# Four more weight granules by seven products, x loaded in pairs, and the first granules laid out piece by piece, in a one-core decoder layer

## The chip, the core and the metric

The kernel runs on one core of a Trainium2 chip. Five engines run their own instruction streams and wait for each other only where a semaphore says so: PE (TensorE, matrix products into PSUM banks; its weight loads are shown as PEld), DVE (VectorE), ACT (ScalarE), POOL (GpSimd) and SP (SyncE, which issues most of the DMAs). The metric is the device time of one launch in microseconds (us); lower is better. A difference below about 0.2% (1.3 us here) can't be told from no change.

## The reference

One layer for 256 tokens of width 2048, float32 throughout. A normalised x is multiplied by one wide input matrix, whose columns are cut into q, k, v, z_a (attention, 8 heads of 128), u_b, v_b, z_b (a gated unit) and two gates:

```python
h = rms_norm(x, norm_g)
proj = h @ w_in
q, k, v, z_a, u_b, v_b, z_b, g_a, g_b = jnp.split(proj, cuts, axis=-1)
q = rms_norm(q.reshape(B, S, N_ATT_HEADS, HEAD_DIM), q_norm_g)
k = rms_norm(k.reshape(B, S, N_ATT_HEADS, HEAD_DIM), k_norm_g)
att = moba_attention(q, k, v)          # 256 tokens: causal attention in one block
y_a = (att * jax.nn.silu(z_a)) @ w_proj_a
sgu = spatial_gating(jax.nn.gelu(u_b), jax.nn.gelu(v_b), sgu_norm_g, w_s, b_s)
y_b = (sgu * jax.nn.silu(z_b)) @ w_proj_b
merged = jax.nn.sigmoid(g_a) * y_a + jax.nn.sigmoid(g_b) * y_b
return x + merged @ w_out
```

Nearly all work is in the products with w_in, w_proj_a, w_proj_b and w_out, some 120 MB of weights that are read once.

## The kernel before

**Granules.** The weights are cut into 120 granules of 128 x 2048 words (1 MB), used in a fixed order (`schedule`): eight granules each for q, k, v, za, vb, ub and zb (numbers 0 to 55), then four times eight for the gates `g` followed by four for the projections `proj`, then twice eight for `out`. In this text g62 is granule 62. A granule of one of the blocks of eight holds, for one pair `kp` of 128-row blocks of the inner dimension, a 2 x 2 grid of weight blocks of 128 x 512. It meets the 2 x 2 grid of x's blocks (two inner blocks, two halves of 128 tokens).

**Halves.** A float32 factor is used as a rounded upper half (type float32r, `wh`, made by ACT) and the rest, the lower half (`wl`, made by DVE as the factor minus its upper half, in place of the raw words). One block product is three matmuls of 128 x 512 (`three`, line 421): lower x by upper weight, upper by upper, upper by lower weight. So the lower half of the weights is first read by a granule's third matmul.

**Eight or seven products.** `direct` does a granule's eight block products: 24 matmuls. `seven` does it by Winograd's form of Strassen's scheme with seven: 21 matmuls. For that the sums of weight blocks have to be made too: DVE makes the block sums (lines 265, 267, 268), ACT their upper halves `th` (L270), and DVE the lower halves `tl` (L273), beside the lower half of the words themselves (L272, for a granule by eight L238). In the blocks of `SCRATCH` the first sum (L265) is made in memory instead: SP copies a quarter of the granule to a `ring` tensor 13 granules ahead, POOL adds another quarter by an accumulating DMA 10 granules ahead, and the quarter is then loaded from the ring. `SETS` holds, for each block, which `kp` go by seven and the order of the eight.

**Banks.** A block keeps its results in two groups of four PSUM banks, `E` (sums that only the sevens make) and `L`. When the last granule by seven is done, `early` empties E (one ACT copy, four DVE additions); when the block is done, `final` empties L (four DVE additions). The next block swaps the two groups.

**Order.** Every engine's order is written out by hand. The loop at line 804 goes over the granules; while PE is given granule i, `LEADS` tells up to which granule the halves are made (i + 2 or i + 3), four buffers hold `wh` (`WHS`), three hold the sums (`TS`, `THS`), six hold raw words (`RAWS`). All else (norms, softmax, transposes, evacuations) hangs on a granule and a place in its step: "pre" is before the halves, "mid" and "late" are inside the making of the halves, "evac" and "post" behind them (`HOOKS`, `EVAC`, and `SECOND` for the second part of a transposition). An instruction that waits holds up everything behind it on its engine.

**The beginning.** SP issues x's scales and first tile, the first granule in four pieces, and then x and granules 1 to 3 alternately (lines 292 to 306). Granules 0 to 3 lie in memory as rows of 8 KB and come in pieces (four, four, two, two) of 128 rows of 2 KB or 4 KB. `split_x` scales a pair of x's tiles and makes its halves. `load_nat` loads x once more, by rows, for the mean squares (`stats`); `forms_4`, `forms_5`, `forms` make the sums of x's blocks that the sevens need, for kp 4, kp 5, and kp 0 to 3; `halves_4` makes the halves of those of kp 4.

Of the kernel before, what the change touches and what calls it, by code (L numbers as in the profile page):

```python
# [22 lines left out]
P = 128  # L23
# [7 lines left out]
WORDS = 2048  # L31
# [12 lines left out]
SETS = {("q", 0): ((), (0, 1, 2, 3, 4, 5, 6, 7)), ("k", 0): ((0, 1, 2, 3, 4), (5, 1, 4, 3, 6, 0, 2, 7)),  # L44
# [7 lines left out]
        ("out", 0): ((0, 1, 2, 4), (3, 0, 2, 6, 1, 5, 4, 7)),  # L52
        ("out", 1): ((0, 1, 2, 3, 4), (5, 0, 1, 2, 3, 4, 6, 7))}
SCRATCH = ("za", "vb", "ub", "zb", "g", "out")
LEADS = {("q", 0): (3, 2, 2, 3, 3, 3, 3, 2), ("k", 0): (2, 3, 3, 2, 2, 2, 2, 2),
# [18 lines left out]
HOOKS = [
# [13 lines left out]
    ("za", 0, 3, "mid", "soft_exp", 0), ("v", 0, 4, "evac", "root", "k", 3), ("zb", 0, 3, "mid", "spatial"),  # L88
    ("ub", 0, 1, "evac", "squares", "vb", 0), ("q", 0, 4, "post", "forms_5"),
    ("za", 0, 5, "post", "soft_sum", 0), ("ub", 0, 3, "evac", "squares", "vb", 1),  # L90
    ("g", 0, 0, "mid", "func", "zb", AF.Silu), ("ub", 0, 5, "post", "norm", "vb", 1),
# [9 lines left out]
    ("za", 0, 3, "post", "soft_max", 1), ("vb", 0, 4, "post", "load_mix"),
    ("ub", 0, 0, "post", "turn_z", "za", "E"), ("proj", 3, 2, "mid", "halves_h", "m"),
    ("vb", 0, 2, "post", "attend", 1, "E23"), ("k", 0, 4, "late", "root", "q", 3),
    ("zb", 0, 2, "mid", "func", "ub", AF.Gelu_apprx_tanh), ("za", 0, 4, "post", "soft_sum", 1),
    ("ub", 0, 4, "evac", "root", "vb", 1), ("g", 0, 5, "post", "gate_b"), ("za", 0, 2, "post", "soft_max", 0),
    ("proj", 2, -1, "post", "func", ("g", 2), AF.Sigmoid), ("proj", 3, 0, "post", "turn_m", 2, (0, 1), "L01"),
    ("proj", 0, 1, "mid", "func", ("g", 0), AF.Sigmoid), ("k", 0, 6, "late", "norm", "q", 3),
    ("proj", 3, 2, "post", "halves_l", "m"), ("proj", 3, 2, "post", "turn_m", 1, (0, 1), "L23"),
    ("out", 0, 0, "in", "turn_m", 3, (0, 1), "E01"), ("out", 0, 2, "late", "forms_m4"),
    ("out", 0, 2, "post", "halves_m4"), ("ub", 0, 1, "mid", "func", "vb", AF.Gelu_apprx_tanh),  # L110
# [27 lines left out]
def hybrid_layer_kernel(  # L138
# [17 lines left out]
    def both(name, words, at):  # L156
# [4 lines left out]
            for i, n in ((0, 4), (1, 4), (2, 2), (3, 2))}  # L161
# [47 lines left out]
    def load_piece(i, a, b):  # L209
        nc.sync.dma_start(raw[i][:, a:b], w[i, :, a:b])  # L210
# [95 lines left out]
    load_x(12, 16)  # L306
# [439 lines left out]
    fns = dict(load_nat=load_nat, keep_vec=keep_vec, forms_4=forms_4, forms_5=forms_5, forms=forms, stats=stats,  # L746
# [33 lines left out]
    def take(i, when):  # L780
        return later.pop((i, when), [])
# [21 lines left out]
    loaded, halved = 3, 1  # L803
    for i, (kind, name, c, kp, n) in enumerate(G):
# [128 lines left out]
```

## Time and profile before

| | us |
|---|---|
| median of 3 runs | 657.42 (657.16 to 658.05) |
| the profiled execution | 657.49 |
| its span on the core | 655.8 |
| PE busy | 648.7 (99%) |
| DVE busy | 595.3 (91%) |
| ACT busy | 433.3 (66%) |
| POOL busy | 81.1 (12%) |

The span runs from the first instruction to the end of the last; the other 1.7 us of the execution lie around it. A busy share is an average over the whole span; the views by window, by wait and in order of time tell what a stage is limited by. In rows of the timeline the columns are start, duration (us), engine, line, operation, result<-operands; consecutive instructions of one engine overlap by some 0.08 us, so that the cost of one is read from start to next start.

### The profile page before, as it was taken

The page shows a single profiled execution, that of the slowest core. Times are in us where ns is not written, and L with a number is a line of the kernel's source. Part 1 is how long each engine was busy: PE and PEld are TensorE (multiplying, and loading weights), DVE is VectorE, ACT ScalarE, POOL GpSimd, SP SyncE. Part 2 cuts the span into 40 slices and gives each one's busy share as a digit, 9 for nine tenths or more (in the row PEclk, how much of TensorE's full clock was granted, in tenths as well). Part 3 has the DMA queues.
Part 4 walks back from the last instruction along what each step waited for, and adds up shares of the span by engine and source line. Part 5 has one row for each costly group of instructions (what it writes and reads, how often), then busy time and mean ns, then how long its engine had stood idle before and what let it go on. Part 6 is the DMA issues. An engine that isn't in the chain of part 4 may idle for free.

```text
span 655.8 us, 8146 instructions
## 1 busy us (share of the span) xinstructions
PE 648.7 (99%) x2968; PEld 536.6 (82%) x2968; DVE 595.3 (91%) x519; ACT 433.3 (66%) x542; POOL 81.1 (12%) x88
## 2 busy tenths in 40 slices
PE   9999999999999999999999999999999999999997
PEld 5787878888888888888888888888888888888885
DVE  4789999979978999979999998899979998999996
ACT  7869778858958678686566755564655476475660
POOL 1000522220010102300011011101101100100300
PEclk9999999999999999999999999999999999999999
DMA  8985596786685976887599679959985997986981
GB/s 298 421 351 212 194 267 228 240 259 184 207 266 156 295 227 210 256 260 283 176 292 288 210 214 320 312 196 277 310 252 193 305 296 207 271 245 223 199 285 64
DMA packets 44824, 163.14 MB, mean 249 GB/s; under 512 B 4977, under 2 KB 5617, under 8 KB 35825
## 3 DMA queue, kind: packets, MB, share of 16 engines
q1 hardware_dynamic: 35280, 145.32, 61.1%
q0 software_dynamic: 8928, 16.26, 16.3%
q10 hardware_dynamic: 576, 1.05, 0.4%
q8 instruction: 23, 0.38, 0.2%
q14 instruction: 17, 0.13, 0.1%
HBM read 157.89 MB, written 28.31 MB: 284 GB/s over the span
## 4 chain that ended last, share of the span: by engine, by line
PE 87%; DVE 6%; DMA 4%; ACT 1%; issue 1%; SPq 0%; DVEq 0%; ACTq 0%
PE acc_g L421 15%; PE y L421 13%; PE seven_g L421 10%; PE acc_out L421 9%; PE acc_vb L421 5%; PE acc_za L421 5%; PE acc_ub L421 5%; PE acc_v L421 5%; PE acc_zb L421 5%; PE seven_out L421 4%; DMA words0float<-in_w 2%; DMA cut_float<-in_w 2%; PE seven_za L421 2%; PE seven_vb L421 2%; PE seven_v L421 2%; PE seven_zb L421 2%
## 5 line engine op out<-in xcount | busy, mean ns | idle before, releaser
L222 POOL DMA_DIRECT2D ring<-in_w x48 | 40.3, 846 | 297.8 <-DMA ring<-in_w 297.6
L270 ACT CAST th<-sums0float 128x1536 fp32r<-128x1536 f32 x19 | 28.2, 1484 | 42.9 <-DVE sums0float L268 42.9
L270 ACT CAST th<-sums1float 128x1536 fp32r<-128x1536 f32 x19 | 28.2, 1484 | 38.6 <-DVE sums1float L268 37.1
L270 ACT CAST th<-sums2float 128x1536 fp32r<-128x1536 f32 x19 | 28.3, 1491 | 32.6 <-DVE sums2float L268 29.4
L421 PE MATMUL acc_g<-wh,xuh 128*128 128x512 f32 x99 | 38.6, 389 | 0.0
L421 PE MATMUL acc_g<-wh,xul 128*128 128x512 f32 x99 | 38.6, 389 | 0.0
L273 DVE TENSOR_TENSOR sums2float32r<-sums2float,th 128x1536 fp32r<-128x1536 f32 x19 | 33.3, 1752 | 2.7 <-ACT th L270 2.7
L238 DVE TENSOR_TENSOR words1float32r<-words1float,wh 128x2048 fp32r<-128x2048 f32 x13 | 29.7, 2285 | 6.3 <-ACT wh L237 6.3
L366 POOL TENSOR_TENSOR rs<-ms,mhalf 128x4 f32<-128x4 f32 x12 | 24.1, 2008 | 86.0 <-DVE ms L365 86.0
L273 DVE TENSOR_TENSOR sums1float32r<-sums1float,th 128x1536 fp32r<-128x1536 f32 x19 | 33.3, 1753 | 0.0
L273 DVE TENSOR_TENSOR sums0float32r<-sums0float,th 128x1536 fp32r<-128x1536 f32 x19 | 33.3, 1752 | 0.0
L238 DVE TENSOR_TENSOR words4float32r<-words4float,wh 128x2048 fp32r<-128x2048 f32 x13 | 29.7, 2287 | 3.7 <-ACT wh L237 3.7
L272 DVE TENSOR_TENSOR words2float32r<-words2float,wh 128x2048 fp32r<-128x2048 f32 x13 | 29.8, 2293 | 1.3
L272 DVE TENSOR_TENSOR words3float32r<-words3float,wh 128x2048 fp32r<-128x2048 f32 x11 | 25.2, 2292 | 4.7 <-ACT wh L260 3.6
L237 ACT CAST wh<-words1float 128x2048 fp32r<-128x2048 f32 x13 | 24.8, 1907 | 3.7 <-PE acc_g L421 3.7
L238 DVE TENSOR_TENSOR words5float32r<-words5float,wh 128x2048 fp32r<-128x2048 f32 x11 | 25.1, 2286 | 1.9 <-ACT wh L237 1.9
L237 ACT CAST wh<-words4float 128x2048 fp32r<-128x2048 f32 x13 | 24.9, 1917 | 1.7 <-PE y L421 1.2
L272 DVE TENSOR_TENSOR words0float32r<-words0float,wh 128x2048 fp32r<-128x2048 f32 x11 | 25.2, 2291 | 0.9
L421 PE MATMUL acc_out<-wh,ml 128*128 128x512 f32 x65 | 25.4, 391 | 0.0
L421 PE MATMUL acc_out<-wh,mh 128*128 128x512 f32 x65 | 25.3, 390 | 0.0
L421 PE MATMUL acc_q<-wh,xuh 128*128 128x512 f32 x64 | 25.1, 392 | 0.2 <-ACT wh L237 0.2
L421 PE MATMUL y<-wh,zal 128*128 128x512 f32 x64 | 25.2, 394 | 0.0
(955 smaller groups left out, 2157.0 us busy)
## 6 DMA issues: line engine op xcount, KB each, us to landing
words4float<-in_w SPq DMA_DIRECT2D x15, 1024.0 KB, 6.6
words1float<-in_w SPq DMA_DIRECT2D x14, 1024.0 KB, 7.4
words5float<-in_w SPq DMA_DIRECT2D x12, 1024.0 KB, 7.3
ring<-in_w SPq DMA_DIRECT2D x48, 256.0 KB, 7.2
ring<-in_w POOLq DMA_DIRECT2D x48, 256.0 KB, 7.4
words3float<-in_w SPq DMA_DIRECT2D x10, 1024.0 KB, 6.6
words0float<-in_w SPq DMA_DIRECT2D x9, 1024.0 KB, 6.3
words2float<-in_w SPq DMA_DIRECT2D x11, 768.0 KB, 6.4
```

Of the source, the lines that this page charges most:

```text
L222: nc.gpsimd.dma_start(pre[i], w[i, :, 2 * B:3 * B], accum_op=ALU.add)
L237: nc.scalar.copy(h, r)
L238: nc.vector.tensor_tensor(l, r, f(h), op=ALU.subtract)
L270: nc.scalar.copy(th[i], t)
L272: nc.vector.tensor_tensor(wl[i], r, f(wh[i]), op=ALU.subtract)
L273: nc.vector.tensor_tensor(tl[i], t, f(th[i]), op=ALU.subtract)
L366: nc.gpsimd.tensor_tensor(dst, ms[:, :n], mhalf[:, :n], op=ALU.pow)
L421: nc.tensor.matmul(acc, a, b, start=(start and n == 0), stop=(stop and n == 2))
```

## The change

- v, za and zb: five, five and six of eight granules go by seven products where it was four each, four more in all; the orders of kp in v, za, zb, and more slightly in k, vb, g and out, are others. The last granule of v and of za is now one by seven.
- The first loads are a list, `LOADS`: x's tiles come two pairs at a time (256 KB) at most, and granules 4 and 5 are issued ahead of x's last pair.
- Granules 0 to 3 are laid out in memory piece by piece on the host (`weight_stream`), so that each piece is one contiguous stretch; `load_piece` reads it so. The rows that arrive in SBUF are the same.
- `split_x` of the later pairs is hung on granules 0 to 3 as hooks; `load_nat` goes from behind granule 4's halves to granule 3; `forms_4` goes ahead of granule 7's halves, `forms_5` behind granule 8's.
- `LEADS`, `EVAC`, `SECOND` and the other `HOOKS` have new values: among them, the sums of v leave at the next block's first granule, and `mix`'s second part goes from "pre" to "mid".

```diff
-SETS = {... ("k", 0): ((0, 1, 2, 3, 4), (5, 1, 4, 3, 6, 0, 2, 7)),
-        ("v", 0): ((0, 1, 2, 3), (4, 5, 0, 6, 1, 2, 3, 7)), ("za", 0): ((0, 1, 2, 3), (4, 5, 0, 1, 6, 2, 3, 7)),
-        ("zb", 0): ((0, 1, 2, 3), (5, 4, 1, 0, 6, 2, 3, 7)),
-        ("g", 0): ((0, 1, 2, 3, 4), (5, 6, 3, 2, 0, 1, 4, 7)),
...
+SETS = {... ("k", 0): ((0, 1, 2, 3, 4), (5, 1, 3, 4, 6, 0, 2, 7)),
+        ("v", 0): ((0, 1, 2, 3, 4), (7, 6, 5, 4, 0, 2, 1, 3)),
+        ("za", 0): ((0, 1, 2, 3, 4), (6, 5, 3, 2, 0, 7, 4, 1)),
+        ("zb", 0): ((0, 1, 2, 3, 4, 5), (6, 1, 4, 5, 3, 2, 0, 7)),
+        ("g", 0): ((0, 1, 2, 3, 4), (5, 6, 0, 2, 4, 3, 1, 7)),
...
-         ("v", 0): (3, 2, 2, 2, 3, 3, 2, 2), ("za", 0): (2, 2, 2, 2, 2, 3, 3, 2),
-         ("zb", 0): (2, 3, 2, 2, 2, 2, 2, 2), ("g", 0): (2, 2, 3, 3, 3, 2, 2, 2),
+         ("v", 0): (2, 3, 3, 3, 3, 3, 2, 2), ("za", 0): (2, 2, 3, 3, 3, 2, 2, 2),
+         ("zb", 0): (2, 2, 2, 3, 3, 3, 2, 2), ("g", 0): (2, 2, 3, 2, 3, 2, 2, 2),
...
-        ("v", 0, "quad"): (0, "mid"),
-        ("za", 0, "early"): (1, "pre"),
+        ("v", 0, "quad"): (1, "pre"),
+        ("za", 0, "early"): (0, "pre"), ("za", 0, "quad"): (1, "pre"), ("ub", 0, "quad"): (1, "late"),
...
-SECOND = {... ("mix", 0): (1, "pre"),
+SECOND = {... ("mix", 0): (1, "mid"),
...
+    ("q", 0, 0, "pre", "split_x", 2), ("q", 0, 0, "pre", "split_x", 3),
+    ("q", 0, 1, "evac", "split_x", 5), ("q", 0, 2, "post", "split_x", 6), ("q", 0, 3, "mid", "split_x", 7),
+    ("q", 0, 1, "mid", "split_x", 4),
-    ("q", 0, 4, "post", "keep_vec"), ("q", 0, 4, "post", "forms_4"), ("q", 0, 4, "post", "forms_5"),
+    ("q", 0, 4, "pre", "keep_vec"), ("q", 0, 4, "pre", "forms_4"), ("q", 0, 5, "evac", "forms_5"),
-    ("q", 0, 4, "late", "load_nat"),
+    ("q", 0, 3, "mid", "load_nat"),
...
+LOADS = [("p", 0, 512), ("p", 512, 1024), ("x", 1, 2), ("p", 1024, 1536), ("p", 1536, 2048), ("x", 2, 4),
+         ("w", 1, 4), ("x", 4, 6), ("x", 6, 8), ("w", 2, 2), ("w", 3, 2), ("x", 8, 10), ("x", 10, 12),
+         ("x", 12, 14), ("w", 4), ("w", 5), ("x", 14, 16)]
+CUTS = {0: 4, 1: 4, 2: 2, 3: 2}
...
     def load_piece(i, a, b):
-        nc.sync.dma_start(raw[i][:, a:b], w[i, :, a:b])
+        src = w[i, :, a:b]
+        if i in CUTS:
+            n = WORDS // CUTS[i]
+            j = a // n
+            src = bass.AP(tensor=w.tensor, offset=w.offset + (i * WORDS + j * n) * P + a - j * n,
+                          ap=[[n, P], [1, b - a]])
+        nc.sync.dma_start(raw[i][:, a:b], src)
...
-    load_piece(0, 0, B)
-    load_piece(0, B, 2 * B)
-    load_x(1, 2)
-    load_piece(0, 2 * B, 3 * B)
-    load_piece(0, 3 * B, WORDS)
-    load_x(2, 4)
-    load(1, pieces=4)
-    load_x(4, 8)
-    load(2, pieces=2)
-    load_x(8, 10)
-    load(3, pieces=2)
-    load_x(10, 12)
-    load_x(12, 16)
+    for kind, *a in LOADS:
+        if kind == "x":
+            load_x(*a)
+        elif kind == "w":
+            load(*a)
+        else:
+            load_piece(0, *a)
...
-    for kp in range(1, 4):
-        split_x(kp)
-        if kp < 2:
-            split(kp, 4)
+    split_x(1)
+    split(1, 4)
...
-    loaded, halved = 3, 1
+    loaded, halved = 5, 1
...
-        if i < 4:
-            split_x(i + 4)
...
+    for i, n in CUTS.items():
+        g[i] = g[i].reshape(P, n, WORDS // n).transpose(1, 0, 2).reshape(P, WORDS)
     return np.ascontiguousarray(np.stack(g))
```

More of the change, by code (lines that the diff above doesn't have):

```diff
@@ L60 @@
+SCRATCH = ("za", "vb", "ub", "zb", "g", "out")
+LEADS = {("q", 0): (3, 2, 2, 3, 3, 3, 3, 2), ("k", 0): (2, 3, 3, 2, 3, 3, 3, 2),
[4 rows of a table added]
          ("g", 3): (2, 2, 2, 2, 2, 2, 3, 3), ("out", 0): (3, 2, 2, 3, 3, 2, 2, 2),
-         ("out", 1): (2, 2, 2, 2, 2, 2, 2, 2), ("proj", 0): (3, 2, 3, 2), ("proj", 1): (3, 2, 2, 2),
+         ("out", 1): (2, 2, 2, 2, 2, 2, 2, 3), ("proj", 0): (3, 2, 3, 3), ("proj", 1): (3, 2, 2, 2),
          ("proj", 2): (3, 3, 3, 2), ("proj", 3): (2, 3, 3, 2)}
-EVAC = {("proj", 0): (1, "late"), ("proj", 1): (1, "late"), ("proj", 2): (1, "late"), ("proj", 3): (0, "evac"),
+EVAC = {("proj", 0): (0, "evac"), ("proj", 1): (1, "late"), ("proj", 2): (0, "evac"), ("proj", 3): (0, "evac"),
@@ L64 @@
         ("g", 2, "quad"): (1, "pre"), ("zb", 0, "early"): (1, "late"), ("out", 1, "quad"): (0, "evac"),
         ("g", 3, "quad"): (0, "evac"), ("k", 0, "early"): (0, "evac"), ("vb", 0, "quad"): (0, "late"),
-        ("v", 0, "quad"): (0, "mid"), ("g", 0, "early"): (0, "late"), ("g", 1, "early"): (0, "evac"),
+        ("v", 0, "quad"): (1, "pre"), ("g", 0, "early"): (0, "late"), ("g", 1, "early"): (1, "mid"),
         ("v", 0, "early"): (0, "pre"), ("out", 1, "early"): (1, "mid"), ("out", 0, "quad"): (0, "late"),
-        ("za", 0, "early"): (1, "pre"), ("g", 3, "early"): (0, "late"), ("q", 0, "quad"): (0, "pre"),
+        ("za", 0, "early"): (0, "pre"), ("g", 3, "early"): (0, "late"), ("q", 0, "quad"): (0, "pre"),
@@ L69 @@
         ("out", 0, "early"): (1, "mid"), ("zb", 0, "quad"): (1, "pre"), ("ub", 0, "early"): (0, "evac"),
-        ("vb", 0, "early"): (0, "evac")}
-SECOND = {("turn_m", 0): (1, "late"), ("turn_m", 2): (1, "post"), ("turn_z", "za"): (1, "late"),
-          ("turn_qk", "q"): (1, "post"), ("mix", 0): (1, "pre"), ("turn_z", "zb"): (1, "post"),
+        ("vb", 0, "early"): (0, "evac"), ("za", 0, "quad"): (1, "pre"), ("ub", 0, "quad"): (1, "late"),
+        ("g", 2, "early"): (0, "late"), ("q", 0, "early"): (1, "late")}
@@ L73 @@
+SECOND = {("turn_m", 0): (1, "mid"), ("turn_m", 2): (1, "post"), ("turn_z", "za"): (1, "mid"),
+          ("turn_qk", "q"): (1, "late"), ("mix", 0): (1, "mid"), ("turn_z", "zb"): (0, "post"),
           ("turn_qk", "k"): (1, "mid"), ("turn_m", 1): (1, "pre")}
 HOOKS = [
[5 rows of a table removed]
-    ("k", 0, 1, "late", "root", "q", 1), ("proj", 0, 0, "late", "turn_z", "zb", "E23L01"),
-    ("k", 0, 1, "pre", "squares", "q", 2), ("k", 0, 3, "late", "root", "q", 2),
-    ("k", 0, 5, "late", "norm", "q", 2), ("k", 0, 3, "pre", "squares", "q", 3), ("zb", 0, 0, "post", "mix", "E"),
@@ L83 @@
-    ("proj", 3, -1, "mid", "turn_m", 0, (0, 1), "E23"), ("v", 0, 0, "mid", "squares", "k", 0),
-    ("v", 0, 1, "evac", "root", "k", 0), ("proj", 3, 0, "evac", "func", ("g", 3), AF.Sigmoid),
[3 rows of a table removed]
[L88 to L91, printed above, removed]
@@ L92 @@
-    ("ub", 0, 3, "evac", "squares", "vb", 2), ("v", 0, 3, "evac", "root", "k", 2),
-    ("ub", 0, 7, "post", "norm", "vb", 2), ("ub", 0, 4, "post", "squares", "vb", 3),
-    ("q", 0, 4, "late", "load_nat"), ("ub", 0, 7, "post", "norm", "vb", 3),
+    ("q", 0, 0, "pre", "split_x", 2), ("q", 0, 0, "pre", "split_x", 3), ("k", 0, 1, "evac", "root", "q", 2),
+    ("q", 0, 1, "evac", "split_x", 5), ("q", 0, 2, "post", "split_x", 6), ("q", 0, 3, "mid", "split_x", 7),
+    ("v", 0, 3, "late", "squares", "k", 3), ("q", 0, 4, "pre", "keep_vec"),
@@ new lines @@
+    ("ub", 0, 2, "pre", "squares", "vb", 0), ("ub", 0, 2, "evac", "squares", "vb", 1),
+    ("q", 0, 5, "post", "forms", "x", "x"), ("vb", 0, 0, "mid", "func", "za", AF.Silu),
[3 rows of a table added]
+    ("proj", 0, 0, "pre", "turn_z", "zb", "E23L01"), ("k", 0, 1, "pre", "squares", "q", 2),
+    ("v", 0, 3, "evac", "root", "k", 3), ("k", 0, 6, "post", "norm", "q", 2),
+    ("k", 0, 3, "pre", "squares", "q", 3), ("zb", 0, 0, "post", "mix", "E"),
+    ("proj", 3, -1, "mid", "turn_m", 0, (0, 1), "E23"), ("za", 0, 3, "mid", "soft_exp", 0),
@@ new lines @@
+    ("ub", 0, 4, "late", "root", "vb", 2), ("za", 0, 5, "post", "soft_sum", 0),
+    ("za", 0, 2, "late", "soft_max", 0), ("v", 0, 1, "late", "root", "k", 1),
+    ("v", 0, 3, "late", "norm", "k", 1), ("v", 0, 2, "late", "squares", "k", 2),
+    ("k", 0, 4, "evac", "root", "q", 3), ("v", 0, 5, "late", "norm", "k", 2),
+    ("v", 0, 0, "mid", "squares", "k", 0), ("q", 0, 1, "mid", "split_x", 4), ("zb", 0, 3, "late", "spatial"),
+    ("proj", 3, 0, "evac", "func", ("g", 3), AF.Sigmoid), ("ub", 0, 3, "late", "root", "vb", 0),
@@ L95 @@
+    ("g", 0, 0, "mid", "func", "zb", AF.Silu), ("ub", 0, 3, "evac", "squares", "vb", 2),
+    ("ub", 0, 6, "evac", "norm", "vb", 1), ("v", 0, 4, "late", "root", "k", 2),
+    ("ub", 0, 0, "post", "turn_z", "za", "E"), ("ub", 0, 3, "post", "squares", "vb", 3),
+    ("q", 0, 3, "mid", "load_nat"), ("q", 0, 6, "evac", "halves_h", "x"), ("ub", 0, 7, "pre", "norm", "vb", 3),
     ("v", 0, 0, "post", "turn_qk", "q", "E"), ("za", 0, 0, "post", "turn_qk", "k", "E"),
-    ("za", 0, 1, "post", "score", "E"), ("q", 0, 6, "post", "halves_l", "x"),
@@ L97 @@
-    ("ub", 0, 6, "post", "root", "vb", 3), ("ub", 0, 1, "mid", "causal_mix"),
+    ("za", 0, 1, "post", "score", "E"), ("q", 0, 6, "post", "halves_l", "x"), ("q", 0, 4, "pre", "forms_4"),
+    ("ub", 0, 5, "evac", "root", "vb", 3), ("ub", 0, 1, "pre", "causal_mix"),
     ("vb", 0, 1, "post", "attend", 0, "E01"), ("za", 0, 4, "mid", "soft_exp", 1),
-    ("ub", 0, 4, "post", "norm", "vb", 0), ("vb", 0, 0, "evac", "turn_p", 0, "E012"),
-    ("vb", 0, 0, "mid", "func", "za", AF.Silu), ("proj", 3, 1, "post", "forms", "mf", "m"),
@@ L101 @@
[L101 to L110, printed above, removed]
+    ("proj", 0, 1, "mid", "func", ("g", 0), AF.Sigmoid), ("vb", 0, 0, "late", "turn_p", 0, "E012"),
+    ("q", 0, 5, "post", "stats"), ("ub", 0, 4, "evac", "norm", "vb", 0), ("za", 0, 3, "late", "soft_max", 1),
@@ new lines @@
+    ("v", 0, 5, "late", "norm", "k", 3), ("ub", 0, 6, "evac", "norm", "vb", 2),
+    ("proj", 3, 2, "mid", "halves_h", "m"), ("vb", 0, 2, "post", "attend", 1, "E23"),
+    ("v", 0, 1, "late", "root", "k", 0), ("zb", 0, 2, "late", "func", "ub", AF.Gelu_apprx_tanh),
+    ("za", 0, 4, "post", "soft_sum", 1), ("ub", 0, 3, "evac", "root", "vb", 1),
+    ("proj", 3, 1, "post", "forms", "mf", "m"), ("q", 0, 8, "post", "halves_4"),
+    ("k", 0, 3, "evac", "norm", "q", 0), ("proj", 2, -1, "post", "func", ("g", 2), AF.Sigmoid),
@@ L111 @@
+    ("proj", 3, 0, "post", "turn_m", 2, (0, 1), "L01"), ("ub", 0, 1, "pre", "func", "vb", AF.Gelu_apprx_tanh),
+    ("k", 0, 6, "post", "norm", "q", 3), ("proj", 3, 2, "post", "halves_l", "m"),
+    ("proj", 3, 2, "post", "turn_m", 1, (0, 1), "L23"), ("out", 0, 0, "in", "turn_m", 3, (0, 1), "E01"),
+    ("out", 0, 2, "late", "forms_m4"), ("out", 0, 2, "post", "halves_m4"), ("g", 0, 5, "post", "gate_b"),
     ("vb", 0, 1, "in", "turn_p", 1, "E301"), ("proj", 1, 0, "mid", "func", ("g", 1), AF.Sigmoid),
-    ("v", 0, 5, "evac", "norm", "k", 3), ("v", 0, 1, "pre", "squares", "k", 1),
+    ("vb", 0, 3, "pre", "load_mix"), ("v", 0, 1, "pre", "squares", "k", 1), ("q", 0, 5, "evac", "forms_5"),
@@ L160, in hybrid_layer_kernel @@
     cuts = {i: [both(f"cut{i}_{j}_", WORDS // n, base + 8 * KB * i + j * 8 * KB // n) for j in range(n)]
-            for i, n in ((0, 4), (1, 4), (2, 2), (3, 2))}
+            for i, n in CUTS.items()}
     class Cut:
@@ L744, in keep_vec @@
         nc.scalar.copy(vec, vec0)
-    fns = dict(load_nat=load_nat, keep_vec=keep_vec, forms_4=forms_4, forms_5=forms_5, forms=forms, stats=stats,
+    fns = dict(split_x=split_x, load_nat=load_nat, keep_vec=keep_vec, forms_4=forms_4, forms_5=forms_5, forms=forms, stats=stats,
                halves_h=halves_h, halves_l=halves_l, halves_4=halves_4, squares=squares, root=root, norm=norm,
@@ L876, in hybrid_layer_kernel @@
             halved += 1
-            split(halved, {1: 4, 2: 2, 3: 2}.get(halved, 1), mid=lambda: run(take(i, "mid"), i), late=lambda: run(take(i, "late"), i))
+            split(halved, {2: 2, 3: 2}.get(halved, 1), mid=lambda: run(take(i, "mid"), i), late=lambda: run(take(i, "late"), i))
         run(take(i, "mid"), i)
         run(take(i, "late"), i)
-        if i < 4:
-            split_x(i + 4)
         run(take(i, "evac"), i)
```

7 lines of the change are left out of this document (3 added, 4 removed), and 23 rows, old and new, of tables (HOOKS, LEADS, SETS).

## The prediction

> **What bounds the kernel now.** I read the busy shares first, then PE's waits, then the chain of work that ended last in order of time.
>
> ```profile
> PE 648.7 (99%) x2968; PEld 536.6 (82%) x2968; DVE 595.3 (91%) x519; ACT 433.3 (66%) x542; POOL 81.1 (12%) x88
> ```
>
> PE is busy all the time by this row, but a matmul that waits half-issued is busy too, so pace has to be read from the chain:
>
> ```profile
> 15.76 13.81 DMA words0float<-in_w
> ...
> 84.50 2.72 PE seven_k L421 x12
> ...
> 93.34 5.44 PE acc_v L421 x24
> ```
>
> Up to about 30 us the end hangs on DMAs (the first row is g6's load); behind that the chain goes through ACT and DVE, which make the weights' halves, and from some 83 us on it is PE to the end. A matmul costs 2.72 / 12 = 0.227 us, so a granule by eight costs PE 24 x 0.227 = 5.44 us and one by seven 21 x 0.227 = 4.76 us. From the first matmul to v's first lie eight granules by eight (q), then five by seven and three by eight (k): 192 + 177 = 369 matmuls, 83.7 us of work.
>
> ```profile
> 5.97 0.50 PE L421 MATMUL acc_q<-wh,xuh 128*128 128x512 f32 x1 [0.17 <-ACT wh L237]
> ```
>
> PE took 93.34 - 5.97 = 87.4 us for them: 3.7 us were lost to late halves. In the window from 83 us to the end PE's waits have one row only:
>
> ```profile
> PE acc_k L421 <- DVE words2float32r L272: 0.5, 1, 0.5
> ```
>
> So from v to the end PE is the bound. That doesn't say that DVE has room. The row of the windows from 208 to 348 us, and the list of DVE's waits from 46.35 us (g9, the first granule by seven) to 348.5 us (g62, next to last of the first gate block), show how close it runs:
>
> ```profile
> 208.40:348.43 140.03, 140.03 (x644) 116.89 (x643) 132.64 (x112) 97.51 (x127) 16.74 (x18) 1.00 0.78 246
> ```
>
> ```profile
> DVE words3float32r L272 <- ACT wh L260: 3.6, 1, 3.6
> DVE v_h L476 <- ACT v_c L475: 3.0, 1, 3.0
> DVE sums2float32r L273 <- ACT th L270: 2.7, 1, 2.7
> DVE words5float32r L272 <- ACT wh L260: 2.6, 1, 2.6
> DVE words4float32r L238 <- ACT wh L237: 1.3, 1, 1.3
> DVE words5float32r L238 <- ACT wh L237: 1.0, 1, 1.0
> DVE za_h L609 <- ACT za_h L607: 0.4, 1, 0.4
> DVE zb_h L483 <- PE acc_zb L421: 0.4, 1, 0.4
> ```
>
> These are 15.0 us of idle time in 302.1. And at g62 DVE is only just in time: it ends the lower half at 346.14 + 2.29 = 348.43, and PE's third matmul reads it at 349.95:
>
> ```profile
> 46.35 0.68 DVE L265 TENSOR_TENSOR words3float<-words3float 128x512 f32<-128x512 f32 x1
> ...
> 346.14 2.29 DVE L272 TENSOR_TENSOR words2float32r<-words2float,wh 128x2048 fp32r<-128x2048 f32 x1
> ```
>
> ```profile
> 349.95 0.39 PE L421 MATMUL acc_g<-words2float32r,xuh 128*128 128x512 f32 x1
> ```
>
> The slack there is 1.52 us. The bound is thus two-fold: PE, with DVE close behind it from g9 to g62.
>
> **The four granules.** PE loses 4 x 3 = 12 matmuls, 12 x 0.227 = 2.72 us. DVE pays for it. From L265 to the next granule's L265 a granule by seven costs it 113.60 - 106.95 = 6.65 us; where the first sum comes by the ring, from L267 to L267, 326.31 - 320.38 = 5.93; one by eight, 312.59 - 310.39 = 2.20:
>
> ```profile
> 106.95 0.69 DVE L265 TENSOR_TENSOR words2float<-words2float 128x512 f32<-128x512 f32 x1
> ...
> 113.60 0.69 DVE L265 TENSOR_TENSOR words3float<-words3float 128x512 f32<-128x512 f32 x1
> ```
>
> ```profile
> 310.39 2.29 DVE L238 TENSOR_TENSOR words2float32r<-words2float,wh 128x2048 fp32r<-128x2048 f32 x1
> 312.59 2.29 DVE L238 TENSOR_TENSOR words3float32r<-words3float,wh 128x2048 fp32r<-128x2048 f32 x1
> ...
> 320.38 0.68 DVE L267 TENSOR_TENSOR sums2float<-words4float 128x512 f32<-128x512 f32 x1
> ...
> 326.31 0.69 DVE L267 TENSOR_TENSOR sums0float<-words5float 128x512 f32<-128x512 f32 x1
> ```
>
> v takes no ring: 4.45 us more. za's one and zb's two do: 3.73 each. Together 15.64 us more DVE work between g9 and g62, and 15.0 us of idle to put it in. ACT gets a `th` of 1536 words for each, at most the 1.91 us of a copy of 2048 words (row below), under 8 us in all beside 42 us of idle time in the window quoted (140.03 - 97.51). SP and POOL issue three ring copies and three adds more; the DMA share there is 0.78, and I cost them at nothing (they are issued ten and more granules ahead; at worst one load comes its own 7 us late).
>
> **The beginning of DVE's chain.** Where DVE starts on g9 decides all that follows. Now `forms_5` follows g7, and ACT's F5h holds g8's copy up behind it:
>
> ```profile
> 24.08 0.33 SPq L210 DMA_DIRECT2D words2float<-in_w  x1
> ```
>
> ```profile
> words2float<-in_w SPq DMA_DIRECT2D x1, 1024.0 KB, 10.4
> ```
>
> ```profile
> 34.88 2.29 DVE L238 TENSOR_TENSOR words1float32r<-words1float,wh 128x2048 fp32r<-128x2048 f32 x1 [0.38 <-ACT wh L237]
> ```
>
> ```profile
> 39.08 0.62 ACT L387 CAST F5h<-F 128x512 fp32r<-128x512 f32 x1 [4.12 <-DVE F L405]
> 39.60 1.91 ACT L237 CAST wh<-words2float 128x2048 fp32r<-128x2048 f32 x1
> 41.41 1.91 ACT L370 ACTIVATE xnat<-xnat 128x2048 f32<-128x2048 f32 x1
> ```
>
> After the change g8's copy needs only its load, which lands at 24.08 + 10.4 = 34.5 (the last number of the issue row), and can start when ACT is free, at 39.08 - 4.12 = 34.96; DVE, through with g7 at 37.1, then does g8 until 39.3, `forms_5` and F5h to 40.9, `forms` to 44.1; ACT's two squares (40.9 to 44.7) run beside it, their x rows being asked for one granule earlier. g9 starts at about 44.75 instead of 46.35: 1.6 us. The bounds are 0 (x's rows or a copy late) and 2.4 (squares hidden wholly). The k order that puts kp 3 ahead of kp 4 takes a wait for `halves_4` away, but k is bound by DVE's chain, so this adds nothing by itself.
>
> **The loads.** Total bytes and their order up to granule 3 are the same; x in pairs lets ACT begin on a pair before the next has come, which I count below as a part of the loads. What the layout does no row shows. The DMA view from 0 to 6 us has a hole where the first pieces should flow:
>
> ```profile
> GB/s 0 0 0 0 0 0 0 0 0 0 0 0 120 165 263 315 288 206 177 137 191 191 191 55 55 14 14 137 150 178 212 287 362 362 348 362 362 355 389 362
> DMA packets 645, 0.94 MB, mean 156 GB/s; under 512 B 66, under 2 KB 322, under 8 KB 645
> ```
>
> From 1.8 us on, 4.2 us at the 390 GB/s of its end would be 1.64 MB; 0.94 MB came: 0.70 MB or 1.8 us lost. If contiguous pieces fill the hole, everything behind the DMA queue (g6's, g7's, g8's loads, and so g9) comes up to 1.8 us earlier; if the hole belongs to the first touch of the memory, nothing changes. Later pieces with the same 8 KB pitch run at 348 and more, which speaks for the second; I take 0.8.
>
> The Trainium skill, page "DMA: Bandwidth & Descriptors", section "Rules for kernel authors", asks for 1 MiB or more in one DMA, and its section "Anatomy of one DMA" has a fixed part of about 2.0 us in each. Paid one behind the other, the two x loads more would make the sum 4 us longer (an estimate from that page). The row just quoted doesn't bear this out: at its end loads of 128 and 256 KB overlap and move 348 to 389 GB/s.
>
> **The sum.** DVE's work from g9 to g62 is 302.1 - 15.0 = 287.1 us. With 15.64 more and the start at 44.75 it ends at 347.5 if DVE never waits. Two waits stay by my reading. One is attend's: DVE waits 0.4 at one of its two groups of products now, and I let it wait at both: 0.75. The other is `mix`: DVE waits 3.6 now because ACT's copy of g51 stands behind mix's part. Hung on "mid", the copy goes ahead, and only `th` stands behind ACT's 3.20 + 1.23 us:
>
> ```profile
> 281.78 3.20 ACT L626 ACTIVATE vb_c<-ps_m,vec 128x128 f32<-128x128 f32 x12 [3.21 <-PE ps_m L617]
> 284.79 1.23 ACT L626 ACTIVATE vb_h<-ps_m,vec 128x128 f32<-128x128 f32 x4
> ```
>
> ACT's part starts some 3 us before DVE is through with L268, so `th` starts 1.5 us late, takes 1.5, and DVE's L272 covers 2.2 of that: about 0.85 is left (bounds 0 and 3.6). So 44.75 + 287.1 + 15.64 + 1.6 = 349.1, PE reads at 349.15 instead of 349.95: 0.8 us gained. PE's own bound is far below: 2.72 + 3.7 = 6.4 us less. DVE's chain therefore takes three quarters and more of what PE would save, as stalls in front of single granules: the last by seven of v, za and zb, and g61 to g62. Behind g62 DVE's work is the same and PE is the bound as before; the new places there (g, out, evacuations) I take as nothing, within 0.5 either way. With 0.8 from the loads the gain is 1.6: 657.49 - 1.6 = **655.9 us**, against the profiled execution, whose span of 655.8 leaves 1.7 around it. That execution is 0.07 above the median of 657.42. A difference under 0.2% (1.3 us) can't be told from none: faster is below 656.1, slower above 658.7.
>
> **The rivals.**
>
> *DVE never waits and the hole is filled.* 347.5 + 0.05 instead of 349.95 is 2.4 us, with 1.8 from the loads 4.2: 653.3. For it: all eight waits are for one engine's order, which the change rewrites. Against: the attend and mix waits depend on PE. The Trainium skill, page "DMA: Bandwidth & Descriptors", section "Latency and other measured facts", has a rule that would fill the hole: copies at large power-of-two row pitches lose bandwidth, and tiles laid out contiguously don't; its smallest listed pitch is 512 KiB, this one is 8 KB, and no run here shows the loss.
>
> *DVE keeps waiting for ACT (slower).* Place: vb to zb. If the waits of 2.6 (vb's first granule by seven, behind the transposed probabilities on ACT) and 3.6 (mix) stay as they are, idle time is 6.2 instead of 1.6 and the end is 4.6 later: 660.5. It decides from 3.2 us of idle on (1.6 + 1.6), and is slower by 0.2% from 4.4 on. For it: with the last granule by seven at the end of v and za, `early` can only start when the block ends, so E's banks come free just before the next block's matmuls need them, and a DVE that is late there holds PE, and PE's late products hold ACT again. Against: DVE falls behind, so that much of what it waited for is there before it comes.
>
> *It does nothing.* Rows in SBUF stay 2 and 4 KB, so the packets are what they were; DVE's start gains 1.6 less and what remains is eaten: 657.5.
>
> **How the numbers follow.** Forecast 0.45, with a range of its own from 654.9 to 657.5 (loads 1.8 or 0, DVE's start 0.8 worse); the first rival 0.22 at 653.3, the second 0.23 at 660.5, the third 0.10. Of the forecast's own range about six tenths lie below 656.1: faster 0.27 + 0.22 = 0.49; same 0.18 + 0.10 = 0.28; slower 0.23. The range reaches from just below the first rival, 653.0, to most of the way to the second, 659.6.
>
> **What would show it.** The matmul count falls by 12; DVE's busy time rises by about 16 us, and its waits between g9 and g62 shrink to a few us. PE's waits gain rows "<- DVE" in v, za, zb and g, with 2 to 5 us in all; if there are none, DVE had room that I didn't see, and the time is under 654. F5h's wait on ACT goes, and the first L265 stands at 44 to 45 us. The hole at 3.5 us is there or not. More than 4 us in rows "DVE <- ACT wh" or "th" means the slower rival.

## The result: slower, and outside the range

| series | kernel | median, us | before on the same chip, us | ratio, 95% interval |
|---|---|---|---|---|
| first | the changed kernel | 662.81 (four executions, from 661.66) | 657.29 (657.15 to 658.05) | 1.0076 [1.0056, 1.0096] |
| e1 | the changed kernel again | 663.94 (661.84 to 664.27) | 657.67 (657.03 to 658.40) | 1.0092 [1.0076, 1.0107] |

The change costs some 6 us; I had forecast a gain of 1.6 us and a range up to 659.6. The profiled execution of the first series took 2332.38 us, with matmuls 157.68 / 192 = 0.82 us apart from the first block on (row below, from its chain of waits) at a granted clock given as 1.000, where the three others took 661.66 to 663.02, so the profile of after is that of e1, an execution of 663.44 us with a span of 661.7.

```profile
10.33 157.68 PE acc_q L429 x192
```

### The profile page after: what moved, and what is told of

Read it like the earlier page. It is cut to its first block, busy times and chain, and to the rows that moved or that the text cites. A ratio compares the mean times of both kernels' runs of the same rounds, so it can differ in the third digit from the quotient of the medians.

```text
span 2330.7 us, 8169 instructions
## 1 busy us (share of the span) xinstructions
PE 2325.1 (100%) x2956; PEld 1242.7 (53%) x2956; DVE 619.4 (27%) x532; ACT 445.1 (19%) x547; POOL 83.5 (4%) x91
## 4 chain that ended last, share of the span: by engine, by line
PE 100%; DVE 0%; DVEq 0%; issue 0%
PE acc_g L429 15%; PE y L429 14%; PE seven_g L429 10%; PE acc_out L429 9%; PE acc_q L429 7%; PE acc_ub L429 5%; PE acc_vb L429 5%; PE acc_v L429 4%; PE acc_za L429 4%; PE acc_k L429 4%; PE seven_out L429 4%; PE acc_zb L429 4%; PE seven_zb L429 3%; PE seven_za L429 2%; PE seven_k L429 2%; PE seven_v L429 2%
## 5 line engine op out<-in xcount | busy, mean ns | idle before, releaser
L429 PE MATMUL acc_g<-wh,xuh 128*128 128x512 f32 x99 | 108.9, 1100 | 0.0
L429 PE MATMUL acc_g<-wh,xul 128*128 128x512 f32 x99 | 107.8, 1089 | 0.0
L429 PE MATMUL acc_out<-wh,ml 128*128 128x512 f32 x65 | 71.7, 1103 | 0.0
L429 PE MATMUL acc_out<-wh,mh 128*128 128x512 f32 x65 | 71.2, 1096 | 0.0
L429 PE MATMUL acc_q<-wh,xuh 128*128 128x512 f32 x64 | 71.1, 1111 | 0.0
L429 PE MATMUL y<-wh,zbh 128*128 128x512 f32 x64 | 70.3, 1098 | 0.0
L429 PE MATMUL y<-wh,zah 128*128 128x512 f32 x64 | 70.3, 1098 | 0.0
L429 PE MATMUL y<-wh,zbl 128*128 128x512 f32 x64 | 69.7, 1090 | 0.0
L429 PE MATMUL acc_q<-wh,xul 128*128 128x512 f32 x64 | 69.5, 1086 | 0.0
L252 DVE TENSOR_TENSOR words5float32r<-words5float,wh 128x2048 fp32r<-128x2048 f32 x12 | 27.5, 2290 | 119.4 <-ACT wh L251 119.4
L284 ACT CAST th<-sums0float 128x1536 fp32r<-128x1536 f32 x20 | 29.4, 1472 | 153.8 <-DVE sums0float L282 153.8
L284 ACT CAST th<-sums1float 128x1536 fp32r<-128x1536 f32 x21 | 30.9, 1473 | 130.2 <-DVE sums1float L282 111.1
L284 ACT CAST th<-sums2float 128x1536 fp32r<-128x1536 f32 x20 | 29.4, 1472 | 102.7 <-DVE sums2float L282 94.4
L429 PE MATMUL acc_g<-words3float32r,xuh 128*128 128x512 f32 x43 | 47.2, 1098 | 0.0
L286 DVE TENSOR_TENSOR words2float32r<-words2float,wh 128x2048 fp32r<-128x2048 f32 x13 | 29.8, 2292 | 51.5 <-ACT wh L274 33.8
L287 DVE TENSOR_TENSOR sums2float32r<-sums2float,th 128x1536 fp32r<-128x1536 f32 x20 | 35.1, 1753 | 27.4 <-ACT th L284 27.4
```

Source lines behind the costliest of these rows:

```text
L252: nc.vector.tensor_tensor(l, r, f(h), op=ALU.subtract)
L284: nc.scalar.copy(th[i], t)
L286: nc.vector.tensor_tensor(wl[i], r, f(wh[i]), op=ALU.subtract)
L287: nc.vector.tensor_tensor(tl[i], t, f(th[i]), op=ALU.subtract)
L429: nc.tensor.matmul(acc, a, b, start=(start and n == 0), stop=(stop and n == 2))
```

## The profile after

Busy shares and the granted clock in 40 slices, from the page of e1:

```profile
PE 649.1 (98%) x2956; PEld 534.6 (81%) x2956; DVE 610.5 (92%) x532; ACT 438.6 (66%) x547; POOL 89.7 (14%) x91
...
PEclk9999999999999999999999999999999999999989
```

12 matmuls fewer, as the change says, DVE 15.2 us busier, and the clock lower in one slice near the end. The line numbers have moved: the sums are L279, L281 and L282 now, `th` L284, the lower halves L286 and L287, and those of a granule by eight L252.

**Up to g62 nothing is lost.** The list of DVE's waits between the first sum of g9 and the lower half of g62, and the timeline's rows at both ends with PE's first product of the projections:

```profile
DVE sums1float32r L287 <- ACT th L284: 1.4, 1, 1.4
DVE v_h L484 <- ACT v_c L483: 0.7, 1, 0.7
DVE ms L373 <- ACT xnat L378: 0.6, 1, 0.6
DVE za_h L617 <- PE ps_a L611: 0.4, 1, 0.4
```

```profile
44.78 0.69 DVE L279 TENSOR_TENSOR words3float<-words3float 128x512 f32<-128x512 f32 x1
...
347.50 2.29 DVE L286 TENSOR_TENSOR words2float32r<-words2float,wh 128x2048 fp32r<-128x2048 f32 x1
```

```profile
349.85 0.50 PE L429 MATMUL acc_g<-words2float32r,xuh 128*128 128x512 f32 x1 [0.89 <-DVE words2float32r L286]
...
359.72 0.39 PE L429 MATMUL y<-wh,zal 128*128 128x512 f32 x1
```

Eight waits with 15.0 us have become three with 2.5 (the third of the list, for ACT's squares, ends at 44.70, just ahead of g9); DVE starts on g9 at 44.78, and PE now stands waiting for it at g62. The projections begin at 359.72, where before they began at 359.70: nothing won and nothing lost so far, though the start of DVE's chain and its idle time came out close to the forecast.

**The loss lies in out's second block.** The chain of waits of e1, asked from 620 us on (start, duration, what):

```profile
615.66 7.74 DMA out_h<-in_x
...
623.41 0.33 SPq L726
...
623.91 0.33 SPq L243
```

```profile
624.29 10.43 DMA words3float<-in_w
...
634.84 0.70 DVE sums1float L281
...
636.89 2.30 DVE words3float32r L286
639.20 0.04 issue
639.24 1.90 PE acc_out L429 x4
641.14 3.61 PE seven_out L429 x12
```

Read from below: PE waits for g117's halves, DVE for g117's load, and that load could not be issued before 624.29 because SP, which issues in order, stood at L726 with the last of four writes of out's first half, and that write waited for POOL's DMA that adds x to it (issued at 615.66, landed 7.74 us later). That in turn began with `early` of out's first half. The same four steps before (DVE, POOL, SP's write, g117's load, and last DVE's first use of that load), and then the four after:

```profile
604.66 0.69 DVE L476 TENSOR_TENSOR out_h<-seven_out,out_c 128x512 f32<-128x512 f32 x1 [0.38 <-PE seven_out L421]
```

```profile
605.76 0.90 POOL L717 DMA_DIRECT2D out_c<-in_x  x1 [28.20 <-DVE out_h L476]
```

```profile
617.75 0.33 SPq L718 DMA_DIRECT2D out<-out_h  x1
...
618.62 0.45 SPq L210 DMA_DIRECT2D words3float<-in_w  x1
```

```profile
631.39 0.69 DVE L267 TENSOR_TENSOR sums0float<-words3float 128x512 f32<-128x512 f32 x1
```

```profile
608.02 2.29 DVE L252 TENSOR_TENSOR words5float32r<-words5float,wh 128x2048 fp32r<-128x2048 f32 x1
610.23 0.68 DVE L484 TENSOR_TENSOR out_h<-seven_out,out_c 128x512 f32<-128x512 f32 x1
```

```profile
611.32 0.91 POOL L725 DMA_DIRECT2D out_c<-in_x  x1 [32.17 <-DVE out_h L484]
```

```profile
623.41 0.33 SPq L726 DMA_DIRECT2D out<-out_h  x1
...
624.29 1.09 SPq L224 DMA_DIRECT2D words3float<-in_w  x1
```

All four are 5.6 to 5.7 us late. `early` of the first out block has the place (1, "mid"): one granule behind the block's last by seven, inside the making of the halves of g113, the second granule of the next block. The change swapped that next block's first two granules, (5, 0, ...) to (0, 5, ...): g112, now by seven (5.92 us of DVE, 602.10 to 608.02), stands ahead of `early`, and g113, now by eight, makes its own lower half (608.02) first.

What it costs PE, in e1's timeline, and the clock in the windows (columns: busy times of PE, PEld, DVE, ACT, POOL, then the granted clock, the DMA share and GB/s):

```profile
636.78 0.50 PE L429 MATMUL acc_out<-wh,ml 128*128 128x512 f32 x1 [0.64 <-ACT wh L274]
637.11 0.40 PE L429 MATMUL acc_out<-wh,mh 128*128 128x512 f32 x1
639.24 0.62 PE L429 MATMUL acc_out<-words3float32r,mh 128*128 128x512 f32 x1 [1.73 <-DVE words3float32r L286]
639.66 0.63 PE L429 MATMUL acc_out<-wh,F5l 128*128 128x512 f32 x1
...
642.65 0.51 PE L429 MATMUL seven_out<-wh,F5h 128*128 128x512 f32 x1
```

```profile
636.40:639.40 3.00, 0.89 (x3) 0.46 (x4) 2.90 (x3) 1.80 (x2) 0.00 (x0) 1.00 1.04 298
639.40:642.90 3.50, 3.50 (x9) 2.72 (x10) 2.86 (x2) 1.90 (x1) 0.00 (x0) 0.51 1.01 347
```

Two waits, 2.8 us by pace, and then eight matmuls 0.427 us apart at half clock, 1.7 us more; with the 0.3 us that PE is behind at the start of out's second block this is the 4.8 us by which g119, the last granule, begins later (650.71 against 645.88). The last 1.1 us lie behind the last product: the final sums are late too, and three of their writes leave within 1.5 us of each other instead of 1.4 us apart.

## The experiments

Start of the first product of some blocks, us from the span's start, and the span, each from one profiled execution:

| | v | zb | g | proj | out | g119 | span |
|---|---|---|---|---|---|---|---|
| before | 93.18 | 275.19 | 319.58 | 359.70 | 569.50 | 645.88 | 655.8 |
| e1, changed | 91.61 | 273.59 | 318.38 | 359.72 | 569.60 | 650.71 | 661.7 |
| e3b, out's old order | 90.87 | 272.85 | 317.89 | 359.24 | 569.09 | 645.65 | 655.5 |
| e6, out's old order, zb four by seven | 90.65 | 272.65 | 317.04 | 357.16 | 566.99 | 643.54 | 653.2 |
| e7, out's old order, zb five by seven | 91.15 | 273.13 | 316.84 | 356.96 | 566.80 | 643.36 | 652.9 |

All four changed kernels reach v 1.6 to 2.5 us sooner than before. From v to zb every row of the table takes the same 182.0 us, and from the projections to out 209.8 or 209.9; they part between zb and the projections and behind out's start.

**e1: the changed kernel again.**

> The changed kernel once more, for a profile in which PE runs at its usual pace (in the one taken, a matmul took 0.8 us instead of 0.227 from beginning to end). Theory A (the slower rival: PE waits for DVE's halves, and DVE for ACT, in v, za, zb and g): 661.5 to 663 us, a pace of 0.227 us per matmul, and 8 to 10 us of PE waits, most of them behind 100 us and marked DVE. Theory B (a lower TensorE clock in these runs, nothing of the schedule): PE's waits no more than the 3.7 us of before, the pace over 0.228 us, and a time under 656 in a run at the clock of before. Theory C (the banks come free late at v to za and za to vb, since the last granule there is by seven): the waits stand at the first matmuls of za and vb, 2 us or more at each.

663.94 us; its profile is the one above, and none of the three theories fits it. A: PE's waits behind 100 us come to 4.6 us, half of them in out, not to 8 to 10 us. B: behind v's start the pace is 0.227 us but for eight matmuls near the end, and no execution came under 661. C: there is no wait over 0.1 us at the first matmuls of za and vb.

**e3 and e3b: out's second block in the old order.**

```diff
-        ("out", 1): ((0, 1, 2, 3, 4), (0, 5, 1, 2, 3, 4, 7, 6))}
+        ("out", 1): ((0, 1, 2, 3, 4), (5, 0, 1, 2, 3, 4, 7, 6))}
```

> The changed kernel with one edit: out's second block takes kp 5 and then kp 0 again, as before the change (its last two stay 7, 6). Theory D (the loss is made behind g103: with kp 0 by seven first, DVE makes a granule by seven and one by eight, some 8.1 us, ahead of the first out block's `early`, instead of one by eight, so the read-and-add DMAs, SP's writes and, behind them on SP, g117's load come 5 to 6 us late): `early` starts near 605 instead of 610.2, g117's load is issued at 618 to 619 instead of 624.3, PE has no wait over 0.5 us behind 600 us, the TensorE clock stays at full speed up to the end, and the time is 656.3 to 658.0. Theory A (the loss comes from DVE's halves in v, za, zb and g): 661.5 to 663.5 as without the edit.

> The kernel of e3 once more, for a profile at the usual clock. Theory (the loss is out's second block): no wait of TensorE over 0.5 us behind 600 us, g117's load issued at 618 to 619 us as before the change, the granted clock full to the end, and the waits of about 1 us at g53, g54 and g62 still there; 656.5 to 658 us. Rival (the loss is spread, or comes from zb alone): waits of TensorE behind 600 us as in the changed kernel, 662 us.

657.39 us, 0.9992 [0.9982, 1.0001], and in e3b 656.97, 0.9992 [0.9982, 1.0002]: the whole loss is gone by this one swap. In e3b g117's load is issued where it was before:

```profile
618.19 0.57 SPq L224 DMA_DIRECT2D words3float<-in_w  x1
```

Its only waits of PE over 0.5 us behind the warm-up are those in zb and g (0.9 us each), and the clock is full to the end.

**e4: the changed kernel, `early` ahead of g113's halves.**

```diff
-         ("out", 0, "early"): (1, "mid"),
+         ("out", 0, "early"): (1, "pre"),
```

> The changed kernel with the changed order kept, but the first out block's `early` hung on the place before g113's halves instead of inside them: it leaves 2.2 us of DVE's work (g113, by eight) of the some 8.1 ahead of it. Theory D: `early` starts near 608, g117's load is issued some 2 us earlier, at about 622, PE's wait at g117 shrinks from 2.4 us to about 1 or less, and since the TensorE clock then need not fall, the time is 658 to 660.5, between the changed kernel and the one with the order back. Theory A: 661.5 to 663.5.

659.37 us, 1.0031 [1.0018, 1.0043]: `early` at 606.70, g117's load at 619.41 (both sooner than expected), a wait of PE of 0.5 us there where the changed kernel had 0.64 and 1.73. Two thirds of the loss are gone. The rest is not SP's order alone: g117's load is issued only 0.8 us later than before, but takes 11.9 us to land where it took 9.1 (last number of each row, before first), and g119's takes 21.4 where it took 16.2.

```profile
words3float<-in_w SPq DMA_DIRECT2D x1, 768.0 KB, 9.1
```

```profile
words3float<-in_w SPq DMA_DIRECT2D x1, 768.0 KB, 11.9
```

So g119's load lands at 641.98 (before 635.97), and behind the last product DVE still has out's sums to make. That the adds and writes in flight beside them slow these loads is likely, but no run shows it.

**e5: the kernel before, with only that order swapped.**

```diff
-         ("out", 1): ((0, 1, 2, 3, 4), (5, 0, 1, 2, 3, 4, 6, 7))}
+         ("out", 1): ((0, 1, 2, 3, 4), (0, 5, 1, 2, 3, 4, 6, 7))}
```

> The kernel before with only the first two granules of out's second block swapped (kp 0 by seven first, then kp 5). Theory D: this alone makes g117's load late, as in the changed kernel: issued at 623 to 625, a wait of 2 to 4 us at g117, 660.5 to 663. Theory A: no change, 657 to 658.5.

661.67 us, 1.0063 [1.0048, 1.0078]: the swap alone makes the kernel before slow. g117's load is issued at 623.44, as expected, but PE's wait for it is 1.0 us and not 2 to 4; most of the time is lost at the end: g119's load lands at 643.44, its halves are made at 645.48, and the sums of out come behind them. There is no half clock in it.

**e9: the changed kernel, the four writes issued by POOL behind its adds.**

```diff
                 nc.gpsimd.dma_start(e[j], part(x, c, j), accum_op=ALU.add)
-                nc.sync.dma_start(part(out, c, j), e[j])
...
+        if c == 0:
+            for j in range(4):
+                nc.gpsimd.dma_start(part(out, c, j), e[j])
```

> The changed kernel with one edit: the four writes of out0's residual sums (L726) are issued by POOL behind its four adds, no longer by SP, so that SP has nothing in front of the last three granules' loads but their buffers. Theory (the loss is SP's order): although early is as late as in the changed kernel, at some 610 us, g117's load is issued by 613 us instead of 624.29 and lands by 627; no wait of TensorE over 0.5 us behind 600 us, no half clock, a tail of about 4.7 us; 656.5 to 658 us like the kernel with the old order. Rival (the late adds themselves crowd the DMA engines, whoever issues the writes): g117's load lands after 632 us, TensorE waits over 1 us there, 660.5 us or more.

656.71 us, 0.9989 [0.9980, 0.9998]. The adds are as late as in the changed kernel, but SP has nothing to stand at:

```profile
611.35 0.91 POOL L725 DMA_DIRECT2D out_c<-in_x  x1 [32.86 <-DVE out_h L484]
```

```profile
612.08 0.43 SPq L224 DMA_DIRECT2D words3float<-in_w  x1
```

The load lands at 619.23, and PE has no wait over 0.1 us behind 600 us. So the late sums by themselves cost nothing: it is the writes' place ahead of three loads on SP that turns them into lost time. What the same adds and writes do to loads that are issued beside them, as in e4, e9 doesn't show, since its first two loads go out ahead of most of them.

**e2: the kernel before with only granules 0 to 3 laid out piece by piece** (`CUTS`, `load_piece` and `weight_stream` of the change).

> The kernel before with one part of the change alone: granules 0 to 3 laid out piece by piece. If contiguous pieces fill the hole at 3.3 to 4.5 us in the DMA view, the first weight piece lands near 3.7 instead of 5.28 us, the first product starts near 4.7 instead of 5.97, and the time is 655.5 to 656.6. If the hole belongs to the first touch of the memory, the first product stays at 5.9 to 6.0 and the time within 0.3 us of the kernel before. My prediction took 0.8 of 1.8 us.

656.71 us, 0.9986 [0.9977, 0.9995]: 0.9 us by the medians, 0.3 to 1.5 by the interval. Neither of the two expectations fits: the first product starts at 5.57, between 4.7 and 5.9, and this 0.4 us is all that the one profiled execution shows. The DMA view from 0 to 6 us still has the hole, narrower and sooner over, and 1.29 MB instead of 0.94 come:

```profile
GB/s 0 0 0 0 0 0 0 0 0 0 0 0 90 120 218 316 247 124 8 249 355 410 423 410 300 328 382 383 348 321 321 321 396 382 396 355 355 355 355 328
```

**e6 and e7: out's old order, and in zb four or five granules by seven instead of six.**

```diff
-        ("zb", 0): ((0, 1, 2, 3, 4, 5), (6, 1, 4, 5, 3, 2, 0, 7)),
+        ("zb", 0): ((0, 1, 2, 3), (5, 4, 1, 0, 6, 2, 3, 7)),         # e6
+        ("zb", 0): ((0, 1, 2, 3, 4), (5, 6, 1, 4, 3, 2, 0, 7)),      # e7
```

> The changed kernel with out's order back and zb as before the change (four by seven, its old order): 6 more matmuls (1.36 us of PE) and 7.46 us less for DVE. My prediction's chain (DVE ends g62's halves just when PE wants them): the waits at g53, g54 and g62 (0.6, 1.2 and 1.2 us, 2.9 together) go, 1.36 comes back, so 1.0 to 2.0 us below the kernel with only the order back: 655.0 to 656.8. If instead each granule by seven is worth its matmuls, this one is 1.4 us slower than that.

> The kernel of e6 with zb's set at five granules by seven instead of four. Chain theory: in e6 VectorE reached g62, ub's granule by seven, with a slack of 1.52 us, so one more granule by seven in zb costs VectorE 3.73 us more there against 0.68 us of matmuls saved (3 x 0.227), with some of the idle time of VectorE in zb and ub to draw on: between 0.3 below e6 and 1.5 above it, 655.0 to 656.7 us where e6 stays at 655.2. Rival, each granule by seven is worth its matmuls: 0.68 below e6, 654.5 us or less.

Six 656.97 (e3b), four 655.18 (0.9966 [0.9954, 0.9979]), five 654.2 (0.9956 [0.9940, 0.9973]). The intervals of four and five overlap, so that the times alone don't show the fifth to gain. The traces do: from zb's first product to that of the projections PE takes 84.51 us before and in e6, 83.83 in e7 and 86.39 in e3b. The fifth gains 0.68 us, its three matmuls, where the chain theory of e7 gave it 0.3 at most; the sixth costs 2.6 there and 2.8 by the medians. (g62, which the expectation of e7 puts in ub, is a granule of the first gate block.) At five, DVE's lower half of g62 is ready 0.41 us ahead of PE, and at six PE waits for it; the rows are those of e7, DVE first:

```profile
344.51 2.29 DVE L286 TENSOR_TENSOR words2float32r<-words2float,wh 128x2048 fp32r<-128x2048 f32 x1
```

```profile
347.21 0.39 PE L429 MATMUL acc_g<-words2float32r,xuh 128*128 128x512 f32 x1
```

The table says the same: e3b loses its lead of 2.3 us between zb (272.85 against 275.19) and the projections (359.24 against 359.70), e7 has one of 2.1 at zb and 2.7 at the projections. e7 is faster than both kernels.

**e8: e6, with v and za by four as before.**

> The kernel of e6 with v's and za's sets put back to four granules by seven each as well, so that of the change only the pairs of x's tiles, the contiguous first granules and out's own sets stay. If the fifth granule of v and of za is each worth its matmuls (3 x 0.227 = 0.68 us), this is 1.36 us slower than e6: 656.5 us. If VectorE's time ate them, it is e6 within 0.3, 655.2 us, or less.

659.14 us, 1.0025 [1.0014, 1.0036], 4.0 over e6, where the matmuls say 1.36: neither expectation. Besides what the expectation lists, the new places (`LEADS`, `EVAC`, `HOOKS`) stay too, and PE's waits show why the run can't be read as the price of two granules:

```profile
PE acc_za L429 <- ACT v_c L483: 1.5, 1, 1.5
...
PE acc_v L429 <- DVE words5float32r L252: 0.5, 1, 0.5
```

The old orders of v and za meet the new places of the evacuations (v's sums now leave at the next block's first granule), and PE is 2.2 us behind e6's pace between the two blocks; with the 1.36 of the matmuls that is all of the 3.5 us that it loses from v to vb. Four granules each with places that fit them is what the kernel before has; these are the first products of v and of vb, before and in e6:

```profile
93.18 0.39 PE L421 MATMUL acc_v<-wh,xul 128*128 128x512 f32 x1
...
183.70 0.39 PE L421 MATMUL acc_vb<-wh,xul 128*128 128x512 f32 x1
```

```profile
90.65 0.39 PE L429 MATMUL acc_v<-wh,xul 128*128 128x512 f32 x1
...
181.16 0.39 PE L429 MATMUL acc_vb<-wh,xul 128*128 128x512 f32 x1
```

90.52 and 90.51 us: in the traces the fifth granules of v and za won nothing, although PE has 1.36 us less to do. e6 gives it back in small pieces, the largest two at attention's scores: they take 5.82 us (145.95 to 151.77) instead of 5.30, and PE stands 0.3 us ahead of them. Whether the fifth granules bring these or the new places do, no run shows.

**e10: e7 with e9's edit.**

> The kernel of e7 with the same edit. It has no wait of TensorE behind 600 us to win back, so the theory gives e7's 654.2 within 0.5 us. Rival: the writes are later on POOL's queue, the late adds with them, and the end hangs on those: 655 us or more.

654.47 us, 0.9958 [0.9941, 0.9975], the same as e7: with the old order SP's writes delay nothing that is needed.

## Why the prediction was wrong

- **The step that failed** is the last one before the loads in the sum: "Behind g62 DVE's work is the same and PE is the bound as before; the new places there (g, out, evacuations) I take as nothing, within 0.5 either way." It measured +5.9 us (level at the projections, 661.7 against 655.8 at the end). DVE's work there is the same, but its order isn't, and I priced the new places by DVE's time alone. SP's and POOL's queues I priced in zb alone, not behind `early` in out, on which POOL's adds, SP's writes and the last three loads hang. The rows were there before: SP's write at 617.75 stood 0.87 us ahead of g117's load, and DVE read that load (landed 627.74) at 631.39, with 3.6 us to spare for a delay that came to 7.
- **The beginning of DVE's chain**: right without the loads' part, 44.78 against 44.75; with it g9 should have started at 43.95.
- **DVE's work and idle time**: from 44.78 to 347.50 + 2.29 = 349.79 are 305.0 us; less 2.5 idle, the work was 302.5 where I had 287.1 + 15.64 = 302.7. The idle time is 2.5 where I had 1.6, and not where I had it: at `mix` (282 us) and at one of attend's two groups there was none, the other kept its 0.4, and of waits that I had dropped two stayed in part, 1.4 of vb's first granule by seven (at 196.87) and 0.7 of v's copy (133.68). PE therefore read g62 at 349.85, 0.1 us earlier than before, not 0.8.
- **The loads**: 0.8 lies within what e2 measured (0.3 to 1.5), although the hole was only narrowed. In the profile of e1 the first product came 0.9 us sooner (5.09), but DVE reached g9 only behind ACT's squares (wait of 0.6, ending at 44.70); in those of the other runs with the changed beginning that start lies from 43.81 to 44.87. x comes in single pairs of tiles, 256 KB each, not two pairs as the list of the change has it. The Trainium skill, page "DMA: Bandwidth & Descriptors", section "Anatomy of one DMA", gives the fixed part of about 2.0 us that I quoted for DMAs that GpSimd issues; x's loads are issued by SP.
- **Without this loss** (e3b, e9) the change gains 0.08% and 0.11%, some 0.5 to 0.7 us (the first interval doesn't exclude none) where I had 1.6. The forecast's mechanism shows in it (a DVE chain that ends at g62 decides), but the chain's term came to nearly nothing.
- **Stalls in front of single granules** were right in zb and g (rows "<- DVE" of 0.9, 0.9 and 0.3 us in e1) and wrong in v and za, where no wait was over 0.3. There the saving went all the same, in the small pieces named under e8, which the sum has no term for. That DVE's chain takes more than PE saves holds for zb's sixth granule, which costs 2.8 us on balance. The reading that PE loses time up to v (3.5 us by v's first product at 93.18; I took 3.7 from the chain's 93.34) was the useful one: there the changed kernels win what they win, apart from zb's fifth granule.
- **The slower rival** had the right sign and the wrong place. Its waits for ACT between vb and zb came to 1.4 us, not 6.2, and e3 shows that its mechanism had no part in the loss.

## What to carry to other kernels

An order change that leaves every engine's work as it is can still delay a load: follow each step that is moved through what it releases (here DVE, POOL's add, SP's write) to the first load queued behind it, and compare that load's slack with the delay. Keep writes that wait for something off the queue that issues the loads, or put them on a queue with nothing behind them. And before adding work to an engine that runs just ahead of the bound, add it a granule at a time: here zb's fifth paid for itself, zb's sixth cost four times what its matmuls saved, and those of v and za won nothing in the traces.

## What the runs showed of the hardware

- After matmuls that began 1.03, 0.33 and 2.13 us apart (the last at 639.24), the granted clock fell to half for 3.4 us (639.24 to 642.65, row 0.51 above). In e4 and e5 a distance of 0.92 and one of 1.40 us brought no such drop: behind them the next matmul came 0.34 us later, and the following ones at 0.227. The Trainium skill, page "TensorE: Matmul & The Clock Gate", section "What's actually happening", gives the half clock after at least one idle window of about 3.4 us and a return after a busy one of as long. The return agrees with this trace (3.4 us); the fall came here with less, since no matmul started more than 2.13 us behind the one before it.
- The hole in the first microseconds of the DMA view is there with contiguous pieces too (8 GB/s in its lowest slice of 0.15 us), but its lowest slices are over at 2.85 us instead of 4.05.
